# Three of four pairs of pool tiles with 84 products of 260 columns in place of 96, from sums of u kept in DRAM

## The chip, the cores and the metric

The kernel runs on one core of a Trainium2 chip. A core has five engines that run side by side, each with its own queue of instructions: PE (matrix products), DVE (vector work), ACT (scalar functions and casts), POOL and SP; the last two issue most of the DMA transfers. Weights and inputs lie in DRAM, tiles in the on-chip SBUF (128 partitions), products in PSUM. The metric is the device time of one execution in microseconds (us).

## The reference

One layer of a hybrid decoder trunk works on 528 positions (16 learned ones, then 512 tokens) of 1024 channels. The normalized input is u. Its product with w_in gives the pool branch (1024 channels), the inputs of a Mamba-2 scan, and the gates. What the change touches is the pool branch: four groups of 256 channels, each averaged over its own window of past positions, minus the channel itself, then mixed by a 256 x 256 matrix:

```python
POOL_WINDOWS = (2, 4, 8, 16)
...
ug = u.reshape(bsz, seqlen, POOL_GROUPS, POOL_GROUP_DIM)
for g, win in enumerate(POOL_WINDOWS):
    xg = ug[:, :, g, :]
    cs = jnp.cumsum(xg.astype(jnp.float32), axis=1)
    ...
    mean = (cs - shifted) / count
    outs.append(mean.astype(u.dtype) - xg)
pooled = jnp.stack(outs, axis=2)
y = jnp.einsum("blgc,gcd->blgd", pooled, w_group)
```

In this text "u" inside pool_mixer is the product of the normalized input with the first 1024 columns of w_in; outside of it u is the normalized input itself. The scan's output and the pool's are each projected to 1024 channels, gated, added, multiplied by w_o, and followed by a squared-ReLU MLP and a last normalization.

## The kernel before

**Arithmetic.** All products are of fp32 accuracy: each operand is split into a high part (a cast to fp32r) and a low part (the rest), and each product is three matmuls, high by high, high by low, low by high. The weights come as blocks of 128 x 1024 (512 KB): `block` (L82) loads one on SP's queue into `raw` (three buffers), ACT casts it to `whi` (L79), DVE subtracts to get `wlo` (L80). `whi` and `wlo` have four buffers each, shared by all blocks in turn. u lies in SBUF as `uh` and `ul`, eight tiles of 128 channels each (k = 0 to 7). `proj` (L155) makes one output tile of 128 channels from one block: for each k the high weights by uh and ul, in two halves of the positions, then the low weights by uh: 8 x 2 x 3 = 48 matmuls.

**Order of the work.** The engines' order is set by the code's order as a scheduler has arranged it with its own costs; the order that results was read from the instruction list. The stages: projections of the first scan group; eight groups of the scan (`ssd`, L423), each woven step by step (`weave`, L553) with the projections of the next; the pool stage; the merge of the two branches (L775 on); w_o; MLP. Each scan group loads `abc`, 1 MB, on POOL's queue (L431).

**The pool stage (L628 to L695).** `pool_tile` (L628) makes one tile: the 48 matmuls into `pp` (PSUM, 258 to 264 columns a half, since a window of w needs w - 1 positions before the first token), a copy to SBUF by ACT (`pu`), additions of the tile to itself shifted by 1, 2, 4, ... (L641, DVE), the scaling and subtraction (L643), and the split of the result into `ph` (ACT, L647) and `pl` (DVE, L648). A group has two tiles, a pair. `pool_mix` (L651) multiplies a pair by the group's 256 x 256 weights (12 matmuls of 512 columns into `pg`), and splits the outcome into `yph` (ACT, L661) and `ypl` (DVE, L662). The groups go in the order 3, 2, 1, 0 (windows 16, 8, 4, 2). Between the tiles stand what fills PE: the last part of the scan's projection (`psl`, L676 to L679, whose sums DVE adds to `acc`), `gate_pool(7)` (L562) and the first `gate_ssd` (L666). Two groups share one block of mixing weights (`wgb`), which stays in its whi and wlo buffers while they last.

**The merge** (L775 on) loads, in each of its first six rounds, one block of w_o into SBUF (`wo_load`, L752) ahead of its other blocks, makes the next gate and the pool's up-projection `pup`, and forms gated sums on DVE.

PSUM: two buffers of two banks for the wide products (`psum2`), four of one bank for the narrow ones (`psum1`).

Of the kernel before, what the change touches and what calls it, by code (L numbers as in the profile page):

```python
# [9 lines left out]
F32 = mybir.dt.float32  # L10
# [4 lines left out]
P = 128  # L15
# [30 lines left out]
WARM = 9  # L46


@with_exitstack
def kernel(ctx: ExitStack, tc, xT, x, w, vec, fnw, out):  # L50
# [31 lines left out]
    def block():  # L82
        t = block_tiles()
        block_part(t, slice(0, 1024))
        return t[2:]

    def units():
# [335 lines left out]
    def ssd(g, cur):  # L423
# [6 lines left out]
        abc = gs.tile([P, R, SEQ], F32, tag="abc", name=f"abc{g}")  # L430
        nc.gpsimd.dma_start(abc, acs_d[hs, :].partition_broadcast(P))  # L431

# [69 lines left out]
        for c in range(3):  # L502
            dve.tensor_tensor(st[c + 1], st[c], bc(cdec[:, c, hs], 64), op=ALU.mult)
            dve.tensor_tensor(flat(st[c + 1]), flat(st[c + 1]), pv[c + 1], op=ALU.add)
        dve.tensor_tensor(dm, dm, cbm.unsqueeze(1).to_broadcast([P, R, 4, P]), op=ALU.mult)
        yield
# [43 lines left out]

    done = {}

# [48 lines left out]
    def out_part():  # L601

        un = units()
        for d in range(NK):
# [3 lines left out]
            yield  # L608

    for g in range(G):  # L610
        nxt = group_tiles(g + 1) if g + 1 < G else None
        fill = [group_proj(g + 1, nxt, GATE_AT.get(g))] if nxt else [out_part()]
        if g == 4:
            fill = [out_half()] + fill
        weave(ssd(g, cur), fill, 2 if g == 4 else 1)
        cur = nxt
    gc_stack.close()


# [3 lines left out]
    gp = pool_stack.enter_context(tc.tile_pool(name="gp", bufs=2, side="left", reuse_waits="tile"))  # L623
    wo_stack = ExitStack()
    wop = wo_stack.enter_context(tc.tile_pool(name="wop", bufs=1, side="right", reuse_waits="tile"))
    yps = {}

    def pool_tile(t):  # L628
        win = WIN[t // 2]
        ps = psum2(f"pp{t}")  # L630

        skip = min(NM - win, NM - 4)
        runs, view = wide(ps, skip)
        proj(runs, block(), U)
        u = gp.tile([P, L], F32, tag="pu", name=f"pu{t}")
        act.copy(u[:, skip:], view)
        s, wdt, lo_ = u, 1, skip
        while wdt < win:
            o = gp.tile([P, L], F32, tag="pw", name=f"pw{t}_{wdt}")
            lo2 = lo_ + wdt  # L640
            dve.tensor_tensor(o[:, lo2:], s[:, lo2:], s[:, lo_ : L - wdt], op=ALU.add)  # L641
            s, lo_, wdt = o, lo2, 2 * wdt
        dve.scalar_tensor_tensor(s[:, NM:], s[:, NM:], 1.0 / win, u[:, NM:],  # L643
                                 op0=ALU.mult, op1=ALU.subtract)
        ph = gp.tile([P, SEQ], F32R, tag="ph", name=f"ph{t}", bufs=3)
        pl_ = gp.tile([P, SEQ], F32R, tag="pl", name=f"pl{t}", bufs=3)
        act.copy(ph, s[:, NM:])  # L647
        dve.tensor_tensor(pl_, s[:, NM:], ph.bitcast(F32), op=ALU.subtract)  # L648
        return ph, pl_

    def pool_mix(gi, pooled, wgb):  # L651
# [14 lines left out]
    def gate_ssd(d):  # L666
# [4 lines left out]
        return gt  # L671

    pend = [pool_tile(2 * POOL_ORDER[0] + i) for i in range(2)]

    un = units()
    for d in range(NK):  # L676
        ps = psum2(f"psl{d}")[:, :SEQ]
        mm3s(ps, [(next(un), ys[k]) for k in (14, 15)])
        dve.tensor_tensor(acc[d], acc[d], ps, op=ALU.add)  # L679
    wgb = block()  # L680
    for n, gi in enumerate(POOL_ORDER):
        nxt = []
        if n < 3:
            nxt.append(pool_tile(2 * POOL_ORDER[n + 1]))
        if n == 0:
            gate_pool(NK - 1)
        if n == 3:
            gts = [gate_ssd(MERGE[0])]
        if n == 2:
            wgb = block()  # L690
        pool_mix(gi, pend, wgb)
        if n < 3:
            nxt.append(pool_tile(2 * POOL_ORDER[n + 1] + 1))
        pend = nxt
    pool_stack.close()  # L695


# [417 lines left out]
def _weight_blocks(i):  # L1115
# [9 lines left out]
    def put(b):  # L1125
        blocks.append(b)
# [34 lines left out]
    blocks += pieces((14, 15))  # L1161
    wg(POOL_ORDER[0] // 2)
    for n in range(4):
        if n < 3:
            put(cols(w_in, 2 * POOL_ORDER[n + 1] * P))
        if n == 0:
            gate(NK - 1)
        if n == 3:
            gate(NK + MERGE[0])
        if n == 2:  # L1170
            wg(POOL_ORDER[n] // 2)
        if n < 3:
            put(cols(w_in, (2 * POOL_ORDER[n + 1] + 1) * P))

# [7 lines left out]
    for n, d in enumerate(MERGE):  # L1182
        if n < len(WO_ORDER):
            wo(*WO_ORDER[n])
        if n + 1 < NK:
            gate(NK + MERGE[n + 1])
        put(cols(w_up, d * P))
    for i in range(2):
        wo("b21", i)
# [62 lines left out]
```

## Time and profile before

| what | us |
|---|---|
| median of 3 runs | 1017.89 (1017.77 to 1018.33) |
| the profiled execution | 1017.65 |
| its span | 1015.9 |
| PE busy | 1007.5 |
| DVE busy | 740.5 |
| ACT busy | 549.1 |
| POOL busy | 10.0 |

The span is the time between the profile's first and last instruction; 1.75 us of the profiled execution lie outside. Engines work at the same time, so busy times don't add up to the span. In lines of groups the columns are: line, engine, operation, output<-input with shapes, xcount | total busy us, mean ns of one | idle us ahead of them and what ended it. In lines of the timeline: start, duration, engine, line, operation, and in brackets the idle time just before and what ended it. Matmuls overlap, so what one costs is read from the distance of starts, not from its duration.

### The profile page before, as it was taken

Reading aid. Unit: us, or ns where it says so; the run is one execution under the profiler, and the core shown is the slowest. Engines: PE = TensorE matmul, PEld = TensorE weight load, DVE = VectorE, ACT = ScalarE, POOL = GpSimd, SP = SyncE. Lnnn points to the kernel's source line nnn. Section 1 sums busy time; section 2 is a strip of 40 time slices with the busy share of each in tenths; the row PEclk is TensorE's granted clock in tenths of the full one; section 3 lists DMA queues with packets and bytes.
Section 4 is the critical chain, followed back from the end, with each engine's and each line's share of the span. In section 5 each row is a group of like instructions: output and inputs, shape, how many; then the busy total and the mean of one; then the engine's idle time right before and its main releaser. Section 6 shows DMA issues by size and latency. Waiting matters only on the chain.

```text
span 1015.9 us, 14095 instructions
## 1 busy us (share of the span) xinstructions
PE 1007.5 (99%) x5697; PEld 869.4 (86%) x5697; DVE 740.5 (73%) x988; ACT 549.1 (54%) x725; POOL 10.0 (1%) x24
## 2 busy tenths in 40 slices
PE   9999999999999999999999999999999999999997
PEld 8889899999889999978999888888888888888886
DVE  7988787777746587887766457887676686676866
ACT  8675958585727339553244333465545455354444
POOL 0100000000000000000000001000000000000000
PEclk9999999999999999999999999999999999999999
DMA  7242242414233231414432334133333323324112
GB/s 249 80 164 84 63 145 63 145 35 154 79 100 113 83 105 42 158 52 138 172 96 91 105 97 151 42 117 133 104 100 108 104 83 125 103 84 125 42 42 84
DMA packets 29715, 105.64 MB, mean 104 GB/s; under 512 B 3345, under 2 KB 4689, under 8 KB 28625
## 3 DMA queue, kind: packets, MB, share of 16 engines
q1 hardware_dynamic: 26928, 92.75, 28.7%
q0 software_dynamic: 2000, 11.08, 2.9%
q8 instruction: 45, 0.74, 0.3%
q10 hardware_dynamic: 720, 0.91, 0.3%
q14 instruction: 22, 0.17, 0.1%
HBM read 102.55 MB, written 2.16 MB: 103 GB/s over the span
## 4 chain that ended last, share of the span: by engine, by line
PE 96%; DVE 2%; ACT 1%; DMA 0%; issue 0%; SPq 0%; ACTq 0%
PE px L161 11%; PE alpha L1000 6%; PE pf L98 6%; PE pf L97 6%; PE pf L100 6%; PE px L163 6%; PE pz L161 5%; PE alpha L1003 3%; PE pp L161 3%; PE pgp L161 3%; PE pgs L161 3%; PE pz L163 3%; PE py L518 2%; PE pso L97 2%; PE pp L163 1%; PE pgp L163 1%
## 5 line engine op out<-in xcount | busy, mean ns | idle before, releaser
L80 DVE TENSOR_TENSOR wlo<-raw,whi 128x1024 fp32r<-128x1024 f32 (+1 forms) x134 | 158.8, 1188 | 123.8 <-ACT whi L79 80.9
L79 ACT CAST whi<-raw 128x1024 fp32r<-128x1024 f32 (+1 forms) x134 | 136.6, 1025 | 202.6 <-PE pf L98 47.0
L161 PE MATMUL px<-uh,whi 128*128 128x264 f32 (+1 forms) x448 | 113.2, 291 | 0.0
L163 PE MATMUL px<-ul,whi 128*128 128x264 f32 (+1 forms) x448 | 110.4, 285 | 0.0
L97 PE MATMUL pf<-vh,whi 128*128 128x512 f32 x256 | 99.8, 390 | 0.0
L98 PE MATMUL pf<-vl,whi 128*128 128x512 f32 x256 | 99.6, 389 | 0.0
L161 PEld LDWEIGHTS px<-uh,whi 128*128 128x128 f32 x448 | 84.6, 189 | 2.2 <-issue 1.5
L163 PEld LDWEIGHTS px<-ul,whi 128*128 128x128 f32 x448 | 84.3, 188 | 0.3
L764 DVE TENSOR_TENSOR slo<-b,shi 128x1024 fp32r<-128x1024 f32 x35 | 42.6, 1218 | 28.8 <-ACT shi L763 15.2
L100 PE MATMUL pf<-vh,wlo 128*128 128x512 f32 x256 | 63.6, 389 | 0.0
L763 ACT CAST shi<-b 128x1024 fp32r<-128x1024 f32 x35 | 36.7, 1050 | 44.9 <-PE pf L98 30.2
L161 PE MATMUL px<-uh,wlo 128*128 128x264 f32 (+1 forms) x448 | 58.5, 283 | 0.0
L100 PEld LDWEIGHTS pf<-vh,wlo 128*128 128x128 f32 x256 | 48.0, 188 | 10.0
L97 PEld LDWEIGHTS pf<-vh,whi 128*128 128x128 f32 x256 | 48.1, 188 | 9.9
L98 PEld LDWEIGHTS pf<-vl,whi 128*128 128x128 f32 x256 | 48.0, 188 | 9.9
L161 PEld LDWEIGHTS px<-uh,wlo 128*128 128x128 f32 x448 | 55.9, 188 | 0.0
L1000 PE MATMUL alpha<-shi,hh 128*128 128x512 f32 x140 | 54.6, 390 | 0.0
L1003 PE MATMUL alpha<-shi,hl 128*128 128x512 f32 x140 | 54.5, 389 | 0.0
L830 DVE TENSOR_TENSOR ht<-ht,alpha 128x1024 f32<-128x1024 f32 x35 | 42.5, 1215 | 15.7 <-PE alpha L1000 15.7
L163 PE MATMUL pz<-ul,whi 128*128 128x512 f32 x112 | 43.6, 389 | 0.0
L161 PE MATMUL pz<-uh,whi 128*128 128x512 f32 x112 | 43.6, 389 | 0.0
L539 DVE RECIPROCAL rs<-rs 128x128 f32<-128x128 f32 x32 | 27.2, 911 | 15.1 <-ACT rs L537 15.1
(415 smaller groups left out, 2330.7 us busy)
## 6 DMA issues: line engine op xcount, KB each, us to landing
raw<-in_w SPq DMA_DIRECT2D x128, 512.0 KB, 3.6
b<-in_w SPq DMA_DIRECT2D x28, 512.0 KB, 3.6
abc<-acs_d POOLq DMA_DIRECT2D x8, 1024.0 KB, 6.2
wob<-in_w SPq DMA_DIRECT2D x8, 512.0 KB, 4.6
xt<-in_xT SPq DMA_DIRECT2D x8, 264.0 KB, 4.7
ht<-in_x POOLq DMA_DIRECT2D x4, 512.0 KB, 5.5
w<-in_w SPq DMA_DIRECT2D x4, 512.0 KB, 3.4
out_dram<-out SPq DMA_DIRECT2D x4, 320.0 KB, 2.5
```

The lines of the kernel that those rows point to most:

```text
L79: act.copy(hi[:, c], raw[:, c])
L80: dve.tensor_tensor(lo[:, c], raw[:, c], hi[:, c].bitcast(F32), op=ALU.subtract)
L97: pe.matmul(ps, ah, bh, start=first and n == 0, stop=False)
L98: pe.matmul(ps, ah, bl, start=False, stop=False)
L100: pe.matmul(ps, al, bh, start=False, stop=last and n == len(pairs) - 1)
L161: pe.matmul(o, wt, rhs[0][k][:, c], start=part == 0 and k == 0, stop=part == 1 and k == NK - 1)
L163: pe.matmul(o, wt, rhs[1][k][:, c], start=False, stop=False)
L763: act.copy(hi, src)
L764: dve.tensor_tensor(lo, src, hi.bitcast(F32), op=ALU.subtract)
L830: dve.tensor_tensor(o, o, src, op=op)
L1000: pe.matmul(ps[t], hh[:, p, seg, st], m, start=bool(first and not low and p == 0), stop=bool(last and low and p == 1), skip_group_check=True)
L1003: pe.matmul(ps[t], hl[:, p, seg, st], m, start=False, stop=False, skip_group_check=True)
```

## The change

Strassen's method (in Winograd's form) makes the product of two matrices, each cut into 2 x 2 blocks, with seven block products in place of eight. Here the left matrix is the weights of a pair (two tiles of 128 channels, the 1024 input channels cut into two halves), and the right one is u (two halves of the input channels, two halves of the positions). The pair of group 3 stays as it was; those of groups 2, 1 and 0 become `pool_pair`: seven products of 4 x 3 = 12 matmuls with 260 columns, 84 for 96. The tokens are cut at 8: positions 8 to 267 and 268 to 527.

The parts:

1. **Weights.** A pair's two blocks are loaded raw. DVE forms four sums of 512 columns, and four forms A, S, D (1024 columns) and B (512) are split into high and low as blocks are, through the same four whi and wlo buffers.
2. **Sums of u.** For each k of 0 to 3, four sums of quarters of u are needed, the same for all pairs. They are formed along the scan, one k in each of the groups 1 to 4: POOL adds high and low parts (two of 128 x 520, behind the group's abc load), DVE does four subtractions of 260 columns, ACT casts twice, DVE makes two lows, and four tiles of 266 KB are written to DRAM on POOL's queue. `ua`, `ub`, `th` and `tl` have one buffer each. After the scan, 16 loads on POOL's queue bring them back into a pool of their own, `tf`.
3. **Combining.** Partial products that several outputs share stay in PSUM (`pxx`, `pyz`) and are copied on the way: ACT does four copies of 260 columns, DVE three additions of 260 columns per pair. `averaged` is the window part of the old pool_tile.
4. **Order.** gate_pool(7) goes ahead of the pairs; the loads of w_o stand behind the gate's and the up-projection's blocks of a round, and their buffers open after the pool stage. The order of the weight blocks in DRAM follows.

By the instruction list PE has 36 matmuls fewer. In the pool stage PE's order after psl is: gate_pool(7), x·A of pair 2, the rest of pool_mix(3), y·A, x·S, z·S, x·D, z·D and x·B of pair 2, y·A and x·A of pair 1, the first two matmuls of pool_mix(2), x·S of pair 1, and so on. A name like x·S2 in the text below is the product into x with form S of pair 2.

```diff
+
+    def raw_block():
+        b = nblk[0]
+        nblk[0] += 1
+        t = wp.tile([P, 1024], F32, tag="raw", name=f"raw{b}", bufs=3)
+        nc.sync.dma_start(t, w[b])
+        return t
+    def split_form(src, c, name):
+        hi = wp.tile([P, 1024], F32R, tag="whi", name=f"whi{name}")
+        lo = wp.tile([P, 1024], F32R, tag="wlo", name=f"wlo{name}")
+        act.copy(hi[:, c], src[:, c])
+        dve.tensor_tensor(lo[:, c], src[:, c], hi[:, c].bitcast(F32), op=ALU.subtract)
+        return hi, lo
...
+    ts_stack = ExitStack()
+    tsp = ts_stack.enter_context(tc.tile_pool(name="tsp", bufs=1, side="right", reuse_waits="tile"))
+    t_d = {(n, p, k): dram.tile([P, 2 * TN], F32R, name=f"t_d{n}{p}{k}")
+           for n in ("13", "42") for p in "hl" for k in range(4)}
+    one, two = slice(0, TN), slice(TN, 2 * TN)
+    def sums_of_u(k, g):
+        a, b = (tsp.tile([P, 2 * TN], F32, tag=t, name=f"{t}{k}") for t in ("ua", "ub"))
+        with tc.issue_after(abc_load[g].ins):
+            for t, kk in ((a, k), (b, k + 4)):
+                pool.tensor_tensor(t, uh[kk][:, SKIP:L].bitcast(F32), ul[kk][:, SKIP:L].bitcast(F32), op=ALU.add)
+        yield
+        with tc.issue_after(masked[g].ins):
+            dve.tensor_tensor(a[:, one], a[:, two], a[:, one], op=ALU.subtract)
+            dve.tensor_tensor(a[:, two], b[:, two], a[:, two], op=ALU.subtract)
+            dve.tensor_tensor(b[:, two], b[:, two], a[:, one], op=ALU.subtract)
+            dve.tensor_tensor(b[:, one], b[:, one], b[:, two], op=ALU.subtract)
+        yield
+        for src, n in ((a, "13"), (b, "42")):
+            hi, lo = (tsp.tile([P, 2 * TN], F32R, tag=f"t{p}", name=f"t{p}{n}{k}") for p in "hl")
+            act.copy(hi, src)
+            dve.tensor_tensor(lo, src, hi.bitcast(F32), op=ALU.subtract)
+            nc.gpsimd.dma_start(t_d[n, "h", k], hi)
+            nc.gpsimd.dma_start(t_d[n, "l", k], lo)
+            yield
...
+        if 0 < g < 5:
+            fill.append(sums_of_u(g - 1, g))
...
-    wo_stack = ExitStack()
-    wop = wo_stack.enter_context(tc.tile_pool(name="wop", bufs=1, side="right", reuse_waits="tile"))
+    tf = pool_stack.enter_context(tc.tile_pool(name="tf", bufs=1, side="left", reuse_waits="tile"))
...
-        s, wdt, lo_ = u, 1, skip
+        return averaged(t, u)
+    def averaged(t, u):
+        win = WIN[t // 2]
+        s, wdt, lo_ = u, 1, min(NM - win, NM - 4)
...
+    def pool_pair(p):
+        a1, a2 = raw_block(), raw_block()
+        sm = tf.tile([P, 1024], F32, tag="sm", name=f"sm{p}")
+        h1, h2, both = slice(0, 512), slice(512, 1024), slice(0, 1024)
+        fa = split_form(a1, both, f"A{p}")
+        dve.tensor_tensor(sm[:, h1], a2[:, h1], a2[:, h2], op=ALU.add)
+        dve.tensor_tensor(sm[:, h2], sm[:, h1], a1[:, h1], op=ALU.subtract)
+        fs = split_form(sm, both, f"S{p}")
+        dve.tensor_tensor(a1[:, h1], a1[:, h1], a2[:, h1], op=ALU.subtract)
+        dve.tensor_tensor(a1[:, h2], a1[:, h2], sm[:, h2], op=ALU.subtract)
+        fd = split_form(a1, both, f"D{p}")
+        fb = split_form(a2, h2, f"B{p}")
+        r1, r2 = (gp.tile([P, L], F32, tag="pu", name=f"pu{2 * p + i}") for i in range(2))
+        n = POOL_ORDER.index(p) % 2
+        x, y, z = pxx[:, 512 * n : 512 * n + TN], pyz[:, :TN], pyz[:, 512 : 512 + TN]
+        c1, c2 = slice(SKIP, SKIP + TN), slice(SKIP + TN, L)
+        u1, u2 = (lambda k: (uh[k][:, c1], ul[k][:, c1])), (lambda k: (uh[k][:, c2], ul[k][:, c2]))
+        form = lambda n, c: lambda k: (T[n, "h", k][:, c], T[n, "l", k][:, c])
+        def product(ps, wf, c, f, start, stop, k0=0):
+            for low in range(2):
+                for k in range(4):
+                    wt = wf[low][:, 512 * c + k * P : 512 * c + (k + 1) * P]
+                    bh, bl = f(k0 + k)
+                    pe.matmul(ps, wt, bh, start=start and not low and k == 0, stop=stop and low == 1 and k == 3,
+                              skip_group_check=True)
+                    if not low:
+                        pe.matmul(ps, wt, bl, start=False, stop=False, skip_group_check=True)
+        product(x, fa, 0, u1, True, False)
+        act.copy(r1[:, c1], x)
+        product(y, fa, 1, u1, True, True, 4)
+        dve.tensor_tensor(r1[:, c1], r1[:, c1], y, op=ALU.add)
+        product(x, fs, 1, form("42", two), False, False)
+        act.copy(r1[:, c2], x)
+        product(z, fs, 0, form("13", one), True, False)
+        act.copy(r2[:, c2], z)
+        yield
+        product(x, fd, 0, form("13", two), False, False)
+        dve.tensor_tensor(r2[:, c2], r2[:, c2], x, op=ALU.add)
+        product(z, fd, 1, u2, False, True, 4)
+        dve.tensor_tensor(r1[:, c2], r1[:, c2], z, op=ALU.add)
+        first = averaged(2 * p, r1)
+        product(x, fb, 1, form("42", one), False, True)
+        act.copy(r2[:, c1], x)
+        yield [first, averaged(2 * p + 1, r2)]
 
...
+    T = {i: tf.tile([P, 2 * TN], F32R, name="t{}{}{}".format(*i)) for i in t_d}
+    for i, t in T.items():
+        nc.gpsimd.dma_start(t, t_d[i])
...
     wgb = block()
+    gate_pool(NK - 1)
+    pxx, pyz = psum2("pxx"), psum2("pyz")
     for n, gi in enumerate(POOL_ORDER):
-        nxt = []
         if n < 3:
-            nxt.append(pool_tile(2 * POOL_ORDER[n + 1]))
-        if n == 0:
-            gate_pool(NK - 1)
+            pair = pool_pair(POOL_ORDER[n + 1])
+            next(pair)
         if n == 3:
             gts = [gate_ssd(MERGE[0])]
         if n == 2:
             wgb = block()
         pool_mix(gi, pend, wgb)
         if n < 3:
-            nxt.append(pool_tile(2 * POOL_ORDER[n + 1] + 1))
-        pend = nxt
+            pend = next(pair)
...
+    wo_stack = ExitStack()
+    wop = wo_stack.enter_context(tc.tile_pool(name="wop", bufs=1, side="right", reuse_waits="tile"))
...
     for n, d in enumerate(MERGE):
-        if n < len(WO_ORDER):
-            wo_load(*WO_ORDER[n])
         if n + 1 < NK:
             gts.append(gate_ssd(MERGE[n + 1]))
         if n >= NK - 2:
             first.append(split(woq["b11", n - NK + 2]))
         ps = psum2(f"pup{d}")[:, :SEQ]
         wh, wl = block()
+        if n < len(WO_ORDER):
+            wo_load(*WO_ORDER[n])
         cs = [slice(k * P, (k + 1) * P) for k in ks]
         mm3s(ps, [((wh[:, c], wl[:, c]), yps[k]) for c, k in zip(cs, ks)])
```

More of the change, by code (lines that the diff above doesn't have):

```diff
@@ L46 @@
 WARM = 9
+SKIP = 8
+TN = (L - SKIP) // 2
 @with_exitstack
@@ L430, in ssd @@
         abc = gs.tile([P, R, SEQ], F32, tag="abc", name=f"abc{g}")
-        nc.gpsimd.dma_start(abc, acs_d[hs, :].partition_broadcast(P))
+        abc_load[g] = nc.gpsimd.dma_start(abc, acs_d[hs, :].partition_broadcast(P))
         xdt = gs.tile([P, 4, R, 64], F32, tag="xdt", name=f"xdt{g}")
@@ L504, in ssd @@
             dve.tensor_tensor(flat(st[c + 1]), flat(st[c + 1]), pv[c + 1], op=ALU.add)
-        dve.tensor_tensor(dm, dm, cbm.unsqueeze(1).to_broadcast([P, R, 4, P]), op=ALU.mult)
+        masked[g] = dve.tensor_tensor(dm, dm, cbm.unsqueeze(1).to_broadcast([P, R, 4, P]), op=ALU.mult)
         yield
@@ L549, in ssd @@
         yield
-    done = {}
+    done, abc_load, masked = {}, {}, {}
     def weave(a, b, n):
@@ L617 @@
     gc_stack.close()
+    ts_stack.close()
     gp_stack = ExitStack()
@@ L1162, in _weight_blocks @@
     wg(POOL_ORDER[0] // 2)
+    gate(NK - 1)
     for n in range(4):
         if n < 3:
-            put(cols(w_in, 2 * POOL_ORDER[n + 1] * P))
-        if n == 0:
-            gate(NK - 1)
+            for i in range(2):
+                put(cols(w_in, (2 * POOL_ORDER[n + 1] + i) * P))
         if n == 3:
@@ L1171, in _weight_blocks @@
             wg(POOL_ORDER[n] // 2)
-        if n < 3:
-            put(cols(w_in, (2 * POOL_ORDER[n + 1] + 1) * P))
     def wo(name, i):
@@ L1182, in _weight_blocks @@
     for n, d in enumerate(MERGE):
-        if n < len(WO_ORDER):
-            wo(*WO_ORDER[n])
         if n + 1 < NK:
@@ L1187, in _weight_blocks @@
         put(cols(w_up, d * P))
+        if n < len(WO_ORDER):
+            wo(*WO_ORDER[n])
     for i in range(2):
```

## Prediction

> **What bounds the kernel now.** I read the page's busy times and chain of waits first, then the list of PE's waits, then the windows of the two stages that the edit touches.
>
> ```profile
> span 1015.9 us, 14095 instructions
> PE 1007.5 (99%) x5697; PEld 869.4 (86%) x5697; DVE 740.5 (73%) x988; ACT 549.1 (54%) x725; POOL 10.0 (1%) x24
> PEclk9999999999999999999999999999999999999999
> PE 96%; DVE 2%; ACT 1%; DMA 0%; issue 0%; SPq 0%; ACTq 0%
> ```
>
> PE is busy for 99% of the span, at full clock in all forty slices, and the chain that ended last is 96% PE. The waits of PE agree, and the two windows show the stages:
>
> ```profile
> PE pdt L203 <- DVE ones_r L108: 1.5, 1, 1.5
> PE psp L97 <- ACT yh L546: 0.9, 1, 0.9
> PE pt_dt L342 <- DVE ddt L331: 0.2, 1, 0.2
> ```
> ```profile
> core 0: us, PE busy (x) PEld busy (x) DVE busy (x) ACT busy (x) POOL busy (x), PEclk, DMA share, GB/s
> 95.00:340.00 245.00, 244.98 (x1618) 219.21 (x1615) 179.67 (x270) 161.45 (x213) 2.65 (x5) 1.00 0.32 103
> 477.00:562.00 85.00, 85.00 (x556) 77.73 (x555) 53.45 (x69) 33.54 (x43) 0.00 (x0) 1.00 0.42 132
> ```
>
> In the whole run PE waits 2.6 us for other engines. In the pool stage (477 to 562 us) it never stops, DVE is busy 53 us of 85, ACT 34. So a matmul removed there is worth its pitch, as long as nothing PE needs comes later. DVE has the second most to do, and the edit gives it work in both stages.
>
> **What is removed.** The pitch of a pool matmul is read from starts: the first of a tile, its last group, and the first of the next work.
>
> ```profile
> 501.52 0.29 PE L161 MATMUL pp<-uh,whi 128*128 128x260 f32 x1
> ...
> 505.36 2.06 PE L161 MATMUL pp<-uh,wlo 128*128 128x260 f32 x16
> 507.26 0.40 PE L161 MATMUL pgp<-uh,whi 128*128 128x512 f32 x1
> ...
> 541.52 0.39 PE L97 MATMUL pg<-ph,whi 128*128 128x512 f32 x1
> 542.89 0.28 PE L161 MATMUL pp<-uh,whi 128*128 128x258 f32 x1
> ...
> 546.68 2.08 PE L161 MATMUL pp<-uh,wlo 128*128 128x258 f32 x16
> 548.60 0.39 PE L161 MATMUL pgs<-uh,whi 128*128 128x512 f32 x1
> ```
>
> A tile of 48 matmuls of 260 columns takes 507.26 - 501.52 = 5.74 us, 0.1196 each; of 258 columns 548.60 - 542.89 = 5.71, 0.119 each; the six 512-column ones from 541.52 to 542.89 take 0.228 each. Pair 2: 96 x 0.1196 - 84 x 0.1196 = 1.44 us saved. Pairs 1 and 0: 96 x 0.119 - 84 x 0.1196 = 1.38 each. **Removed: 4.2 us.** The count of twelve per pair and the pitch are both plain, so 3.9 to 4.2 bounds it. The 12 matmuls of each pool_mix, the gate and the out-part stay; gate_pool(7) only changes place.
>
> **What is added to DVE and ACT in the pool stage.** Here are prices from the stage's own groups (count, then busy total and mean in ns) and, for pitch, from starts that follow each other.
>
> ```profile
> 483.97 1.23 DVE L80 TENSOR_TENSOR wlo<-raw,whi 128x1024 fp32r<-128x1024 f32 x1 [4.07 <-ACT whi L79]
> 485.11 0.70 DVE L641 TENSOR_TENSOR pw<-pu 128x527 f32<-128x527 f32 x1
> 485.84 2.17 DVE L641 TENSOR_TENSOR pw<-pw 128x525 f32<-128x525 f32 x3
> 488.05 0.69 DVE L643 SCALAR_TENSOR_TENSOR pw<-pw,pu 128x512 f32<-128x512 f32 x1
> ...
> 499.28 1.28 DVE L679 TENSOR_TENSOR acc<-acc,psl 128x512 f32<-128x512 f32 x2
> ```
> ```profile
> L662 DVE SCALAR_TENSOR_TENSOR ypl<-pg,vs,yph 128x512 fp32r<-128x512 f32 x8 | 5.9, 747 | 1.0 <-ACT yph L661 1.0
> L504 DVE TENSOR_TENSOR st<-st,pst 128x256 f32<-128x256 f32 x24 | 9.9, 412 | 0.2
> L79 ACT CAST whi<-raw 128x1024 fp32r<-128x1024 f32 x16 | 16.8, 1052 | 38.0 <-PE pp L163 14.6 <-PE psl L98 8.6 <-issue 8.0
> L647 ACT CAST ph<-pw 128x512 fp32r<-128x512 f32 x8 | 5.0, 619 | 7.3 <-DVE pw L643 7.3
> L498 ACT COPY st<-pst 128x256 f32<-128x256 f32 x8 | 2.9, 366 | 1.4 <-PE pst L496 1.4
> ```
>
> A 1024-column low costs DVE 485.11 - 483.97 = 1.14; a 512-column add 0.72 when it follows its own input (2.17 / 3) and about 0.61 when not (1.28 - 0.69 = 0.59 is the second of two adds); a 260-column add from PSUM has no row of its own: the 256-column one lasts 0.41 with its tail, of which about 0.07 overlaps the next, as it does with the two adds; I take 0.34 (0.30 to 0.41). ACT: 1.05, 0.62 and 0.37.
>
> For a pair the old code asked of DVE two 1024 lows, the window sums and the lows of ph and yph. The new one asks: three 1024 lows and a 512 low, 3 x 1.14 + 0.61 = 4.0; four 512 sums of weights, 2.4; three adds of 260, 1.0; window sums, some 3.9 for pair 1; two lows of ph 1.2; two ypl 1.4; one low of the pool weights 1.14 for every second pair. That is 14 to 15 us a pair. PE's share of a pair is now 84 x 0.1196 + 12 x 0.228 = 12.8 us. **So DVE, not PE, is the slower engine over pairs 2 and 1**, and it cannot work ahead freely: whi and wlo have four buffers, and one holds the pool weights of groups 3 and 2 until pool_mix(2), so three rotate. S1's forms (S of pair 1) go where D2's were, D1's where B2's were, B1's where A1's were.
>
> **The largest wait.** I count from the start of y·A2 (t = 0); a product is 12 x 0.1196 = 1.435 us. PE's order, as the instruction list has it: y·A2, x·S2, z·S2 (ends 4.3), x·D2, z·D2, x·B2 (8.6), y·A1 and x·A1 (11.5, with a copy before the second 11.65), then pg2 from ph4, the first averaged tile of pair 2, queued ahead of x·S1. On DVE: the buffer of S2 is free at 4.0, ACT casts A1 (1.05), so A1's low starts at 5.1. From there to ph4's input, in DVE's order: low of A1 1.14, add of x 0.34, two sums for D1 1.21, add of z 0.34, low of S1 1.14, first window sum 0.61: 9.9. Low of D1 1.14 (its cast is done 1.05 after x·B2's last use, 9.65), second window sum 0.61: 11.65. The low of B1 waits for x·A1 to leave its buffer, 11.8, and takes 0.61; third window sum 0.61, the scaling of L643 0.69 and its tail: 13.9. The cast of ph4 on ACT is 0.62: 14.6. **PE waits 14.6 - 11.65 = 2.95 us.** Behind this matmul stand x·S1 and all of pair 1, though they need nothing of ph4; no earlier work is left.
>
> The same list for the next pair: pair 1's window sums are one addition shorter, but its two ypl, delayed by the first stall, stand in front. Resuming at 14.6, PE reaches pg1 from ph2 at 28.6 (six products, two times 0.46 and 2.8 of pg2, then x·A0 and y·A0); DVE's list to ph2 ends between 30.0 and 30.7: a wait of 1.4 to 2.1, I take 1.6. Pair 0's mix has the first gate_ssd in front (24 x 0.228 = 5.5 us): none.
>
> **Smaller new waits.** x of pair 0 is written where pair 1's x·B1 is still being copied, or to the other half of the same tile: a copy of 0.37 and the hand-overs, 0.6 to 0.9, taken 0.75. x·A1 behind a copy 0.15. psl, where adds now stand behind two sums of weights of 0.61 and 0.72, has a wait of 0.29 already on the loading side:
>
> ```profile
> 492.52 0.19 PEld L97 LDWEIGHTS psl<-yh,whi 128*128 128x128 f32 x1 [0.29 <-DVE acc L679]
> ```
>
> I add 0.3. Pool stage: -4.2 + 2.95 + 1.6 + 0.75 + 0.15 + 0.3 = **+1.55**.
>
> **The scan.** In each of groups 1 to 4 DVE gets four subtractions of 260 columns and two lows of 520 (4 x 0.34 + 2 x 0.63 = 2.6 us) and ACT two casts (1.2). Over 245 us that is 10.5 and 5 us on engines with 65 and 83 us free (the first window), so nearly all hides. It isn't free where PE's queue waits on DVE with no slack:
>
> ```profile
> 112.63 0.88 DVE L474 TENSOR_SCALAR abc<-abc,dtok 128x128 f32<-128x128 f32 x4 [3.45 <-ACT eb L466]
> 113.42 0.40 DVE L446 TENSOR_TENSOR xdtm<-ptm,dtm 16x256 f32<-16x256 f32 x1
> ```
>
> DVE runs such stretches back to back. Eight additions of 128x520 go to POOL, whose row nearest to it and that of DVE are
>
> ```profile
> L641 DVE TENSOR_TENSOR pw<-pw 128x517 f32<-128x517 f32 x2 | 1.4, 697 | 0.1
> L110 POOL TENSOR_SCALAR_AFFINE_SELECT tri<-ones_f 128x128 f32<-128x128 f32 x1 | 0.3, 283 | 0.0
> ```
>
> so 0.70 to 0.283 x 520 / 128 = 1.15 each; POOL has nothing else to do, so the adds themselves are hidden. On POOL's queue, though, stand the abc loads too, and now 16 writes of 266 KB:
>
> ```profile
> 236.71 0.53 POOL L431 DMA_DIRECT2D abc<-acs_d  x1 [48.03 <-DVE xc L371]
> 241.49 1.06 ACT L529 ACTIVATE sqg<-yt 128x1024 f32<-128x1024 f32 x1
> ...
> 245.11 0.62 ACT L273 CAST qhg<-sqg 128x512 fp32r<-128x512 f32 x1 [1.85 <-DVE sqg L530]
> ```
> ```profile
> abc<-acs_d POOLq DMA_DIRECT2D x8, 1024.0 KB, 6.2
> out_dram<-out SPq DMA_DIRECT2D x4, 320.0 KB, 2.5
> ```
>
> th and tl have one buffer each, so the cast of t42 waits in ACT's queue until the write of t13 has landed. Nearest prices: 2.5 us (320 KB) and 6.2 (1 MB). In group 3 the cast of t13 stands ahead of sqg, so it ends at about 241.49 + 0.62 = 242.1, and its write goes out behind an abc load: landed at 242.1 + 2.5 = 244.6 or + 6.2 = 248.3, while ACT's next work that PE needs is at 245.11. Late by 0 to 3.2 us; the same again in group 4 at worst. I take the price of the transfer of its size, so 0, and 0.9 for DVE's dense stretches (0 to 1.5: a third of the 2.6 us in one group, or nothing).
>
> The T loads (16 x 266 KB at the page's rates, some 2.5 us each and overlapping) end around 486 us, 25 us before x·S2; the wo loads behind the pool stage still come three or more blocks ahead of their sums. Cost 0; if a T load were late PE would wait for it once, in x·S2.
>
> **Sum.** The profiled execution took 1017.65 us, 1.75 outside its span. -4.2 + 5.75 + 0.9 = +2.45: 1020.1. The median of the runs, 1017.89, lies 0.24 above the profiled one, so 1020.34, **forecast 1020.3 us**.
>
> **Rivals.**
> 1. Faster: DVE keeps up. If the scheduler's order costs less than I count (a low at 1.0 instead of 1.14, or a window sum run before the lows) ph4 and ph2 come in time and the matmuls count in full: 1017.9 - 4.2 + 0.2 of small waits = 1013.9. It decides for faster when all new waits are under 2.1 us. For it: DVE was idle for 31 of 85 us. Against: the idle time lay in waits for buffers, and those are now more.
> 2. The writes land late: 3.2 us at group 3 and up to as much at group 4: 1020.3 + 3 to 6.4, 1023 to 1027. For it: abc's 6.2 us in front on the same queue. Against: the out writes' 2.5.
> 3. POOL's additions hold DVE up. The Trainium skill, "SBUF — State Buffer", section "SBUF: two separate sides", says that DVE with two SBUF inputs and a GpSimd instruction that reads SBUF exclude each other for a whole instruction. As a mechanism here: eight additions of 1.15 us or more would stop DVE for their length in dense stretches; 8 x 1.15 = 9 us, of which perhaps a quarter reaches PE: 1020.3 + 2.3 = 1022.6. The trace has no POOL addition to judge it by. By the cost table of "GPSIMD Engine Reference", section 3.1, one would be an estimated 1.2 us. No run here shows that either.
> 4. The clock drops after the wait of 2.95 us. At the start nine 512-column matmuls run slowly:
>
> ```profile
> 1.51 4.21 PE L203 MATMUL pdt<-ones_r 128*128 128x512 f32 x9 [1.51 <-DVE ones_r L108]
> 5.67 0.89 PE L150 MATMUL px<-xh,whi 128*128 128x264 f32 x2
> ```
>
> They take (5.67 - 1.51) / 9 = 0.46 us each, twice 0.228. Such a stretch of 4.2 us costs 2.1: 1022.4. The Trainium skill, "TensorE: Matmul & The Clock Gate", Part 1, puts the drop behind an idle window of about 3.4 us; by it a wait of 2.95 would not suffice.
>
> **Chances.** Forecast 0.64 (its own range 1018.7 to 1021.7, from the 1.4 to 2.1, the 0 to 1.5 and the small waits); rival 1 0.09; rival 2 0.12; rival 3 0.10; rival 4 0.05. A measurement tells about 0.2% from no change, 2.04 us: faster is below 1015.85, slower above 1019.93. Rival 1 alone is faster: 0.09. Of the forecast's 0.64 some 0.27 lies below 1019.93, so same 0.27, slower 0.64. The range, 1017.8 to 1024.5, leaves out rival 1 and the upper half of rival 2: 0.15 to 0.2.
>
> **What would show it.** In the profile of the changed kernel PE's list of waits should name pg from ph (the cast), 2 to 3 us once and 1 to 2 once, with DVE busy without a gap before it; the 260-column matmuls should keep the pitch of 0.12, with 36 fewer matmuls. A wait on t42's cast or on qhg in groups 3 and 4 would speak for rival 2; DVE additions much over 0.7 us beside POOL's for rival 3; a PEclk digit below 9 near 525 us for rival 4. No wait of PE at pg, and the forecast is wrong in its main term.

## The result and the profile after

The changed kernel takes 1028.01 us (median of 6 runs, 1024.12 to 1030.26) against 1018.0 (6 runs, 1017.58 to 1018.55): ratio 1.0095, 95% interval 1.0075 to 1.0116. It is slower, as forecast, but by 10.0 us and not by 2.4, above the end of the range (1024.5). It also scatters over 6.1 us where the kernel before scatters over 1.0. The profiled execution, 1030.26 us, is the slowest of the six.

The same lines of the page, after:

```profile
span 1028.5 us, 14191 instructions
PE 1010.4 (98%) x5661; PEld 869.4 (85%) x5661; DVE 773.1 (75%) x1039; ACT 559.0 (54%) x746; POOL 38.7 (4%) x64
PEclk9999999999989999999999999999999999999999
PE 46%; ACT 0%; issue 0%; DVE 0%; ACTq 0%
```

There are 36 matmuls fewer (5661 for 5697), yet PE is busy for longer (1010.4 us for 1007.5), and the clock row has an 8 in its twelfth slice. Fewer matmuls and more busy time go together only if some of them ran slower. Six lines of PE's list of waits are new; these are the longest of all, with the four longest new ones among them:

```profile
PE pg L114 <- ACT ph L700: 4.1, 2, 2.8
PE pso L114 <- ACT acc L615: 2.8, 1, 2.8
PE pdt L220 <- DVE ones_r L125: 1.5, 1, 1.5
PE ptx L470 <- DVE xdtm L463: 1.3, 1, 1.3
PE psp L114 <- ACT yh L563: 0.9, 1, 0.9
PE pxx L729 <- ACT pu L749: 0.7, 1, 0.7
```

The first and the last are in the pool stage, and they are the forecast's: 2.8 and 1.3 for ph4 and ph2 (it had 2.95 and 1.6), 0.7 behind the copy (0.75). The second and the fourth are in the scan. The two stages in windows, moved by what lies in front of them:

```profile
95.00:349.00 254.00, 249.50 (x1620) 221.51 (x1617) 197.35 (x294) 166.59 (x222) 22.90 (x29) 0.99 0.36 116
486.00:575.00 89.00, 84.15 (x522) 75.88 (x521) 68.31 (x96) 38.44 (x56) 0.00 (x0) 0.98 0.41 135
```

DVE is now busy for 68 us of 89 in the pool stage. The scan's product py, after the second wait, starts at 286.60 us before and 295.43 after; the first gate behind the pairs at 548.60 and 561.14. So 8.8 us are lost by 295 us, nearly all in the scan (0.4 is a wait at 8 us, in the first projections), and 12.5 - 8.8 = 3.7 behind it, in the pool stage. Before, then after:

```profile
286.60 1.09 PE L518 MATMUL py<-abc,xdt 128*64 128x128 f32 x16
```
```profile
295.43 0.99 PE L535 MATMUL py<-abc,xdt 128*64 128x128 f32 x14
561.14 0.40 PE L178 MATMUL pgs<-uh,whi 128*128 128x512 f32 x1
```

(The line of the gate before, 548.60, stands in the prediction.) Of the 8.8, 3.0 are there ahead of the wait in group 4 (po starts at 283.09 for 280.08), 2.8 are that wait, and 3.0 come behind it.

**The wait in group 4.** The timeline of ACT, then PE, around 280 us:

```profile
278.32 0.63 ACT L651 CAST th<-ua 128x520 fp32r<-128x520 f32 x1
281.51 1.05 ACT L82 CAST whi<-raw 128x1024 fp32r<-128x1024 f32 x1 [2.56 <-PE pso L115]
285.80 0.62 ACT L651 CAST th<-ub 128x520 fp32r<-128x520 f32 x1 [3.23 <-DMA t_d13h<-th]
286.32 0.58 ACT L615 COPY acc<-pso 128x512 f32<-128x512 f32 x1
```
```profile
283.09 1.06 PE L529 MATMUL po<-ct,st 128*128 128x128 f32 x8
286.96 0.80 PE L114 MATMUL pso<-yh,whi 128*128 128x512 f32 x1 [2.81 <-ACT acc L615]
287.55 0.63 PE L115 MATMUL pso<-yl,whi 128*128 128x512 f32 x1
287.98 0.63 PE L114 MATMUL pso<-yh,whi 128*128 128x512 f32 x1
...
293.04 0.39 PE L114 MATMUL pso<-yh,whi 128*128 128x512 f32 x1
```

ACT's second cast of the group waits for the DRAM write of the first, because th has one buffer; behind it in ACT's queue stands the copy that empties pso's PSUM tile, and PE waits for that. The write was issued at 279.25 us and had not landed before 285.7, 6.4 us in all. The forecast took the price of the 320 KB writes, 2.5, and kept 6.2 for a rival, which had the write behind an abc load. Here the last abc load was issued at 239.09, 40 us earlier, so that is not the reason. After the wait the matmuls of 512 columns start 0.43 us apart (287.55, 287.98), not 0.23, until 293.0.

**The clock.** The windows view around the two longest waits; the column behind POOL's is the granted clock:

```profile
280.00:284.00 4.00, 4.00 (x23) 3.40 (x21) 1.88 (x4) 1.05 (x1) 0.53 (x1) 1.00 0.95 259
284.00:287.00 3.00, 0.19 (x3) 0.04 (x1) 1.62 (x3) 1.11 (x2) 0.29 (x1) 0.85 0.61 188
287.00:293.00 6.00, 6.00 (x14) 4.74 (x15) 0.25 (x1) 0.00 (x0) 0.78 (x2) 0.50 0.35 114
531.00:534.00 3.00, 0.17 (x3) 0.00 (x1) 2.62 (x5) 0.67 (x2) 0.00 (x0) 1.00 0.64 176
534.00:537.00 3.00, 3.00 (x17) 2.91 (x18) 3.00 (x6) 0.44 (x2) 0.00 (x0) 0.72 0.51 173
537.00:545.00 8.00, 8.00 (x52) 7.57 (x52) 5.96 (x9) 4.48 (x8) 0.00 (x0) 0.89 0.00 0
```

From 287 to 293 us PE runs at half clock; behind the wait for ph4 part of 534 to 537 and of 537 to 545 does (3 x 0.28 + 8 x 0.11 = 1.7 us lost). In the first stretch it is 3 x 0.15 + 6 x 0.50 = 3.4 us, of which 0.4 falls into the wait itself and 3.0 on matmuls. The page's clock row keeps its 9 at the second stretch: there 1.7 us are lost in a slice of 26, so the digit that the prediction named as a sign is too coarse to show it.

**POOL's additions.** DVE's instruction that runs beside the first two of them, against the same one of the kernel before:

```profile
96.12 1.31 POOL L641 TENSOR_TENSOR ua<-uh,ul 128x520 f32<-128x520 f32 x1
97.39 1.32 POOL L641 TENSOR_TENSOR ub<-uh,ul 128x520 f32<-128x520 f32 x1
...
96.21 3.05 DVE L542 TENSOR_TENSOR yt<-yt,zt 128x512 f32<-128x512 f32 x1
```
```profile
96.10 0.68 DVE L525 TENSOR_TENSOR yt<-yt,zt 128x512 f32<-128x512 f32 x1
```

3.05 us in place of 0.68: the addition ends at 99.26, 0.55 us after POOL's second one (98.71), so it got nearly all of its work done only then, and DVE's whole queue is 2.4 us late. PE's wait of 1.3 us for xdtm comes 18 us later; that the two belong together is tested below (adds on DVE). The Trainium skill, "SBUF — State Buffer", section "SBUF: two separate sides", has the rule as the prediction's third rival told it, and the trace agrees: the two exclude each other for the whole instruction.

### The profile page after: what moved, and what is told of

It is laid out like the page before. It is cut to its first block, busy times and chain, and to the rows that moved or that the text cites. A ratio compares the mean times of both kernels' runs of the same rounds, so it can differ in the third digit from the quotient of the medians.

```text
span 1028.5 us, 14191 instructions
## 1 busy us (share of the span) xinstructions
PE 1010.4 (98%) x5661; PEld 869.4 (85%) x5661; DVE 773.1 (75%) x1039; ACT 559.0 (54%) x746; POOL 38.7 (4%) x64
## 5 line engine op out<-in xcount | busy, mean ns | idle before, releaser
L82 ACT CAST whi<-raw 128x1024 fp32r<-128x1024 f32 (+1 forms) x128 | 130.3, 1024 | 180.9 <-PE pf L115 47.0
L83 DVE TENSOR_TENSOR wlo<-raw,whi 128x1024 fp32r<-128x1024 f32 (+1 forms) x128 | 153.9, 1206 | 99.4 <-ACT whi L82 63.8
L1105 PE MATMUL alpha<-slo,hh 128*128 128x512 f32 x140 | 37.4, 389 | 0.0
```

What stands on the lines that cost most here:

```text
L82: act.copy(hi[:, c], raw[:, c])
L83: dve.tensor_tensor(lo[:, c], raw[:, c], hi[:, c].bitcast(F32), op=ALU.subtract)
L1105: pe.matmul(ps[t], hh[:, p, seg, st], m, start=bool(first and not low and p == 0), stop=bool(last and low and p == 1), skip_group_check=True)
```

## Experiments

Theory A, from the two traces: POOL's additions hold DVE up, the late landing of a write holds ACT up, PE at half clock follows long waits, and the pool stage's waits are the forecast's. Theory B: the additional work of DVE and ACT hides in the scan as forecast, and the pool stage holds the loss. All runs are against the kernel before on the same chip, and the differences below are those from it, since it varies by 0.4 us from chip to chip (the changed kernel: +10.0). The scan and the pool stage were first taken apart.

| kernel | us, median (lowest to highest) | before | ratio, 95% interval |
|---|---|---|---|
| sums alone | 1024.07 (1022.29 to 1024.63) | 1017.58 | 1.0059, 1.0046 to 1.0072 |
| pool alone | 1021.90 (1020.66 to 1022.84) | 1017.58 | 1.0041, 1.0029 to 1.0053 |
| own buffers | 1023.23 (1022.37 to 1023.67) | 1017.58 | 1.0054, 1.0042 to 1.0066 |
| adds on DVE | 1025.95 (1022.16 to 1027.19) | 1017.58 | 1.0076, 1.0063 to 1.0090 |
| scan mended | 1021.62 (1021.09 to 1023.38) | 1017.90 | 1.0040, 1.0027 to 1.0054 |
| mix after s | 1022.60 (1021.36 to 1023.41) | 1017.90 | 1.0047, 1.0034 to 1.0059 |
| filled wait | 1020.97 (1020.59 to 1021.60) | 1017.90 | 1.0031, 1.0020 to 1.0043 |
| mix last | 1022.29 (1022.13 to 1023.07) | 1017.90 | 1.0045, 1.0032 to 1.0058 |
| four pu | 1018.39 (1017.54 to 1018.54) | 1017.76 | 1.0005, 0.9996 to 1.0014 |
| two pairs | 1017.01 (1016.58 to 1017.49) | 1017.76 | 0.9993, 0.9984 to 1.0002 |
| two pairs, groups 1 3 4 5 | 1016.64 (1016.33 to 1017.32) | 1017.74 | 0.9990, 0.9981 to 0.9999 |
| four pu, groups 1 3 4 5 | 1018.38 (1017.87 to 1019.23) | 1017.74 | 1.0007, 0.9998 to 1.0016 |

### Sums alone

The kernel before, with `sums_of_u` along the scan; T isn't loaded and the pool stage is the old one.

> The kernel before with the sums of u formed along the scan and written to DRAM, and nothing that uses them (the loads after the scan are left out, the pool stage is the old one). Theory A: the scan's loss is made of three things that the profile of the changed kernel shows: POOL's eight additions stop DVE for 1.3 to 1.5 us each (some 3 us reach PE), the cast of t42 in group 4 waits for a landing (2.8 us of PE), and TensorE then runs at half rate for one or two windows of 3.4 us (1.7 or 3.4 us lost). So 1024 to 1027 us. Theory B (the forecast's): the extra DVE and ACT work hides but for 0.9 us, and the rest of the loss belongs to the pool stage: 1018.9 us.

1024.07, 6.5 us over before. Theory A's figures hold and B's (1018.9) doesn't: the greater part of the loss is in the scan. The waits of PE in it:

```profile
PE pso L100 <- ACT acc L601: 2.6, 1, 2.6
...
PE ptx L456 <- DVE xdtm L449: 1.3, 1, 1.3
```

Both are those of the changed kernel.

### Pool alone

No sums are formed: the parts of u themselves are written to DRAM in their place, so the products are of the right size and of other numbers.

```diff
     def sums_of_u(k, g):
...
+        for kk, n in ((k, "13"), (k + 4, "42")):
+            nc.gpsimd.dma_start(t_d[n, "h", k], uh[kk][:, SKIP:L])
+            nc.gpsimd.dma_start(t_d[n, "l", k], ul[kk][:, SKIP:L])
```

> The changed kernel without the sums: the parts of u themselves are written to DRAM in the place of the sums (so the products use other numbers), with no work of POOL, DVE or ACT for them. Theory A: the scan loses nothing, the pool stage has -4.2 of matmuls, 4.8 to 5.6 of waits and 1.7 of half rate when a window follows the 2.8 us wait: 1018.6 to 1021.5 us. Theory B: the pool stage holds most of the loss: over 1024 us.

1021.90, 4.3 us over before, 0.4 above A's end and below B's. With the 6.5 of the sums alone that makes 10.8, against 10.0 measured together: the two losses add up to within the scatter, and the pool stage's is the smaller. Its waits are those of the changed kernel, and the clock behind them too (0.97 over 60 us is 1.8 us of full speed):

```profile
PE pg L114 <- ACT ph L687: 4.1, 2, 2.8
...
PE pxx L716 <- ACT pu L736: 0.7, 1, 0.7
```
```profile
500.00:560.00 60.00, 55.20 (x350) 50.26 (x350) 48.10 (x70) 28.90 (x43) 0.00 (x0) 0.97 0.32 101
```

### Own buffers, and adds on DVE

Two edits to the scan, one at a time. Own buffers: th13 and th42 have a buffer each, the lows are formed in place.

```diff
-            hi, lo = (tsp.tile([P, 2 * TN], F32R, tag=f"t{p}", ...) for p in "hl")
+            hi, lo = tsp.tile([P, 2 * TN], F32R, tag=f"th{n}", ...), src.bitcast(F32R)
```

> The changed kernel with a buffer of its own for each of the four tiles that are written to DRAM in a group (the lows are formed in place in ua and ub), so that no cast waits for a landing within a group. Theory A: PE's wait of 2.8 us before pso goes, and with it the half rate behind it (3.4 us): 1020 to 1023.5 us, and the half-rate stretch in the scan is gone from the records. Theory B: the cast was late for other reasons and PE waits as long elsewhere: 1026 to 1029 us.

1023.23, within A's figures: +5.65 for +10.0. No line for pso is left in PE's waits, and the clock stays at 1.00 where the half-rate stretch stood:

```profile
260.00:300.00 40.00, 40.00 (x205) 32.93 (x204) 26.15 (x41) 20.77 (x32) 2.15 (x4) 1.00 0.39 119
```

Adds on DVE: `pool.tensor_tensor` becomes `dve.tensor_tensor` in the first loop of sums_of_u.

> The changed kernel with the eight additions of 128x520 on DVE in place of POOL. Theory A: they cost DVE 8 x 0.61 = 4.9 us in place of the 10 to 11 us for which POOL's stop it, DVE's instructions in the scan keep their usual length (no 3 us ones), and 1 to 2 of the 3 us of small waits go: 1024 to 1027.5 us with the wait in group 4 still there. Theory B: DVE's load is what delays PE, so more of it on DVE costs more: 1028.5 to 1032 us.

1025.95, within A's figures: +8.4 for +10.0, where B had it slower. With more work on DVE the kernel is no slower, and in the median faster, though it scatters by 5 us, so that the 1.6 us between the medians is a rough figure. The instruction beside which POOL worked has its old length, and the line for ptx is gone from PE's waits, while pso's stays:

```profile
96.00 0.68 DVE L542 TENSOR_TENSOR yt<-yt,zt 128x512 f32<-128x512 f32 x1
```
```profile
PE pso L114 <- ACT acc L615: 2.5, 1, 2.5
PE pdt L220 <- DVE ones_r L125: 1.5, 1, 1.5
PE psp L114 <- ACT yh L563: 0.9, 1, 0.9
```

### Scan mended

Both edits together.

> The changed kernel with both edits to the sums at once: the eight additions on DVE, and a buffer of its own for each tile that is written. Theory A: the scan then costs as good as nothing, and what is left is the pool stage as it was alone (+4.3 us): 1021.0 to 1022.5 us, one half-rate stretch of 3.4 us, behind the 2.8 us wait for ph4. Theory B: DVE's and ACT's extra work in the scan costs something by itself: over 1023 us.

1021.62: A's figure, +3.7 for +10.0. But its profile isn't as A had it, in two ways. The scan isn't free: group 4's py starts 1.3 us later than before (287.94 for 286.60; 0.4 of it is the wait at 8 us), and PE's list has a new wait of 1.1 us behind DVE's st (L521). Both edits together make one, for the lows now lie in ua and ub, and DVE's next addition into ua has to wait for the write of the last one to land:

```profile
158.06 0.70 DVE L641 TENSOR_TENSOR ua<-uh,ul 128x520 f32<-128x520 f32 x1 [3.96 <-DMA t_d13l<-ua]
```

In adds on DVE the same addition waits for nothing and there is no wait behind st, which fits; no run tests it. And the profile has the 2.8 us wait for ph4 and no half rate behind it:

```profile
500.00:560.00 60.00, 55.22 (x356) 49.88 (x356) 49.55 (x72) 29.38 (x44) 0.00 (x0) 1.00 0.32 105
```

So a wait of this length may or may not bring the half rate; the last section shows what decides.

### Mix after s, mix last, four pu

Three steps on what bounds the pool stage. The first two queue pool_mix of pairs 2 and 1 later on PE; `mark` is the last matmul of z·S of the next pair in the one, of x·B in the other (which also puts a pair's first window sums behind its last copy in the code):

```diff
+            with tc.issue_after(mark.ins):
                 pool_mix(gi, pend, wgb)
```

> The kernel of scan_mended with the mix of pair 2 (and of pair 1) queued on PE behind z.S of the next pair, 2.9 us later than before. If DVE is the slower engine over the pair, as the forecast says, the wait only moves to ph5, whose list on DVE ends some 3 us behind PE: 1020 to 1022 us, a wait of 2 to 3.5 us for ph5. If only the place of the first two matmuls of the mix was at fault, the waits for ph4 and ph2 go with nothing in their place: 1015.5 to 1017.5 us.

> The kernel of scan_mended with the mix of pair 2 (and of pair 1) queued on PE behind all seven products of the next pair, 7.2 us later than before. If DVE's lag behind PE over a pair is about 2 to 3 us and is made good by the gate's matmuls ahead of pair 0's mix, the waits for ph go: 1017.6 - 4.2 + 1 to 2 of small waits, 1014.4 to 1016.5 us, no half rate. If the forms of weights come late in place of ph (DVE is behind with everything), waits of over 2 us show at the products of pairs 1 and 0: 1018 to 1021 us.

1022.60 and 1022.29: no gain at all. In both the waits for ph are gone and waits of about the same sum stand elsewhere. Mix after s, then mix last:

```profile
PE pxx L729 <- ACT pu L736: 4.6, 2, 3.1
```
```profile
PE pxx L729 <- ACT pu L736: 3.1, 1, 3.1
...
PE pyz L729 <- ACT pu L742: 1.1, 1, 1.1
```

4.6 and 4.2 us in place of 4.1, now for copies of products into pu. The first of the two expectations had named ph5, and neither had named pu; that the wait moves and doesn't go was right. In mix last the copy has the cast of ph4 in front of it on ACT, and that waits for DVE's window sums:

```profile
525.35 0.62 ACT L700 CAST ph<-pw 128x512 fp32r<-128x512 f32 x1 [2.41 <-DVE pw L696]
525.87 0.37 ACT L736 COPY pu<-pxx 128x260 f32<-128x260 f32 x1
```

Four pu gives mix last two more buffers for pu (`bufs=4`).

> The kernel of mix_last with four buffers in place of two for pu, the tiles into which the products are copied. In mix_last PE waits 4.2 us for ACT's copies into pu, which wait until DVE's window sums have read the pair before. If that is only a matter of buffers, DVE's lag is now taken up by them and made good under the gate's matmuls: 1016.5 to 1018.3 us, no wait over 1 us in the pool stage. If DVE has more work than PE in these pairs, the wait moves on, to lows of weight forms or to ph: 1018.5 to 1021 us with waits of 2 us and more.

1018.39, between the two figures: +0.6 for mix last's +4.4. With the four buffers the first copies of the next pair no longer stand behind ph's cast (523.12, ahead of the cast at 525.84), and what remains are waits for DVE itself, none of them near the 2 us that the second figure asked for:

```profile
PE pyz L729 <- DVE pu L738: 0.8, 1, 0.8
PE pxx L729 <- DVE pu L745: 0.6, 1, 0.6
```

So DVE's lag can be taken up by buffers and made good later. The stage from its first psl to the first gate then takes 58.75 us (490.43 to 549.18), for 59.06 before (489.54 to 548.60): 0.3 less, of the 4.2 that were removed.

### Filled wait

Ten matmuls of 512 columns, used nowhere, ahead of pair 2's mix, in scan mended.

> The kernel of scan_mended with ten matmuls of 512 columns (2.3 us of PE, results used nowhere) queued ahead of the first two matmuls of pair 2's mix, where PE waits for 2.8 us. If the half rate follows from PE standing still, the stretch at half rate is gone and the kernel is 1.7 us faster than scan_mended though it does more: 1019.5 to 1020.8 us. If half rate and wait are unrelated, the time is that of scan_mended or up to 0.5 us longer.

1020.97, 0.65 us below scan mended though it does more, but not 1.7: no decision. The highest of the runs came down (1021.60 for 1023.38), which fits half-rate stretches that no longer occur; the lowest came down too (1020.59 for 1021.09), which they don't explain. Neither of the two profiled executions has such a stretch, so they can't be compared for it.

### Two pairs, and other groups for the sums

Two pairs is scan mended with pair 1 by the old pool_tile (and with PSUM tiles of its own for each new pair).

> The kernel of scan_mended with pair 1 made in the old way (96 matmuls, no forms), so that pairs 2 and 0 alone are made from seven products. The old pair asks some 10 us of DVE for 14 us of PE, so DVE makes up its lag of 2 to 3 us there. If the waits come from DVE's lag, the two of them for ph go, and the stage keeps -2.8 us of matmuls: 1016 to 1018 us. If they come from the order of PE's queue and not from DVE's load, one wait of 2 us or more stays at the first matmuls of a mix: 1018.5 to 1021 us.

1017.01, 0.75 us below before (the interval reaches 1.0002). None of the three waits of the pool stage is left, and over 60 us PE stands still for 0.05:

```profile
500.00:560.00 60.00, 59.95 (x387) 54.19 (x387) 46.35 (x65) 30.10 (x43) 0.00 (x0) 1.00 0.41 132
```

The last two kernels form the sums in groups 1, 3, 4 and 5 of the scan (`if g in (1, 3, 4, 5)`).

> The kernel of two_pairs with the sums of u formed along the scan groups 1, 3, 4 and 5 in place of 1, 2, 3 and 4. In two_pairs the scan's only new wait stands in group 2 (po behind DVE's st, 0.6 us, and the row before it). If DVE is without slack there alone, the wait goes: 1016.0 to 1016.8 us, faster than the kernel before. If group 5 is as tight, the wait only moves: 1016.8 to 1017.3 us.

> The kernel of four_pu (all three pairs) with the sums along groups 1, 3, 4 and 5. The same step: 0.6 to 0.9 us less than four_pu's 1018.4, so 1017.5 to 1017.8 us; and, if DVE's load in the pool stage is what eats the third pair's gain, it stays behind the kernel with two pairs by 1 us or more, though it has 12 matmuls fewer.

1016.64 with two pairs, the one kernel that is faster than before beyond its interval (0.9981 to 0.9999, 1.1 us); 1018.38 with three, no change. The reason given was not met: the wait of po is still there, 0.6 us in the first, and so is DVE's wait for a landing (3.5 us at 157), so the step from 1017.01 to 1016.64 isn't explained and is within what two measurements can differ by. With three pairs the kernel is 1.7 us slower though it has 12 matmuls fewer, as expected; but the two also differ in the place of the mix and in the buffers for pu, so that the 1.7 is not the price of the third pair alone.

## Why the prediction was too small

- **What is removed, 4.2 us: right.** The new products keep the pitch: in two pairs the 84 of pair 2 run from 509.17 to 519.90 us, with three matmuls of the mix (0.68) among them, so 10.05 us or 0.1196 each, as forecast. Not all of it arrives: two pairs are worth 2.8, and from the first psl to the first gate the stage takes 57.19 us (490.15 to 547.34) for 59.06, 1.9 less. A wait of 0.3 at psl is part of the difference; the rest is spread over many hand-overs.
- **The pool stage's waits, 5.75 us: right in place and about in size.** 2.8, 1.3 and 0.7 for 2.95, 1.6 and 0.75. That DVE, not PE, is the slower engine over pairs 2 and 1 was argued from counts. Mix after s and mix last bear it out, since the wait moved with its size, and two pairs does the other way round, since with DVE's share lowered the waits are gone. But order and buffers count as well: four pu leaves DVE its work and has no wait over 0.8 us in the stage. Too small were the other small waits, 0.45 in the sum: scan mended's stage, without half rate, is 2.5 us longer than before (61.59 us from the first psl to the first gate), for 1.55 forecast, though its long waits were a little shorter than forecast.
- **The scan, 0.9 us: this step failed.** It measured 8.8 in the profiled execution (with the half rate, 3.0 of it), 6.5 in the median of the sums alone. Two of its statements were wrong. "The adds themselves are hidden" looked at POOL's time alone: DVE pays, 2.4 us for the first two, and some 2 us reach PE (adds on DVE: 1.6 in the median; in the profiled execution PE is 3.0 late ahead of the wait in group 4, from this and other causes). And for the landing, "I take the price of the transfer of its size, so 0": the write in group 4 took 6.4 us, in a stretch where the DMA engines were 95% busy (the window 280 to 284), and PE lost 2.8 us (own buffers). One median was the wrong price for 16 writes whose landings go from 2.3 to 6.4 us; the rival had the 6.2, with a chance of 0.12. Why this one was late isn't shown: the busy engines are an obvious candidate, but in group 3 writes of the same size landed in 3.1 and 3.2 us while the engines were as busy (a share of 0.95 and 0.82, for 0.78 here, each over the time of the write).
- **The clock after the waits: not in the sum, a chance of 0.05.** The changed kernel has 3.4 + 1.7 us of it in the profiled execution. I let the Trainium skill's 3.4 us of idleness talk down waits of 2.8; the runs say otherwise, see the last section. The size, 2.1 for one stretch, was not far off: one of 3.4 us costs up to 1.7, the double one cost 3.0 on matmuls.
- **The rivals were set up as alternatives.** Rivals 2, 3 and 4 came true together, and each had been priced on the forecast alone. (Rival 2 did in its effect, a late landing that holds up ACT, but in group 4 alone and not behind an abc load.) They are linked: the late write is the wait that brings the half rate. Added up at the forecast's own prices, 3.0 + 2.3 + 2 x 2.1 on 1020.3 would have been 1029.8.

What stays open: why the write in group 4 landed late, and the small new hand-overs of the pool stage (1 to 2 us).

## What to carry to other kernels

Moving work to an idle engine isn't free when its instructions keep another from its operands: compare the length of that engine's instructions beside the moved ones. A single buffer that is read by a DMA puts the landing time of the worst moment, not the usual one, into the queue of the engine that writes it next: ACT in the changed kernel, DVE when the lows moved into ua and ub. And when PE is bound, count the other engines per stage: of the kernels tried, the one that gained had two of three pairs made by Strassen's method and less work for DVE in the pool stage.

## What was not expected of the hardware

A wait of 2.5 to 3.1 us can be enough for a stretch at half rate: in the profiles it follows in 8 of 10 such waits, for 3.4 us each but once, when it was twice that (286.1 to 293.0 us). Between the first 8 us and PE's last matmul no profile has one without such a wait. The Trainium skill, "TensorE: Matmul & The Clock Gate", Part 1, names a window of about 3.4 us without work; the stretch has that length, the waits ahead of it were shorter. Such a wait can thus cost 1.4 to 3.0 us of matmul time on top of its length, and a kernel with several of them scatters: the mean granted clock of the changed kernel's runs goes from 0.998 in the fastest (1024.12 us) to 0.994 in the slowest (1030.26), which makes some 4 of the 6.1 us between them.

What decides can be read from the clock records of the traces. Within an execution every change of the clock falls on one grid of 3.413 us (in the changed kernel, 286.13 and 535.30 are 73 steps apart). What counted was how long PE stood still within one step of that grid, and the half rate began with the next step. Here are two steps of the changed kernel, then two of scan mended, around the same wait of 2.8 us:

```profile
531.89:535.30 3.41, 1.30 (x9) 1.22 (x10) 3.30 (x7) 0.89 (x2) 0.00 (x0) 1.00 0.70 249
535.30:538.71 3.41, 3.41 (x19) 3.41 (x17) 2.72 (x5) 0.53 (x2) 0.00 (x0) 0.50 0.10 38
```
```profile
525.01:528.42 3.41, 1.71 (x12) 1.62 (x13) 3.30 (x7) 0.89 (x2) 0.00 (x0) 1.00 0.73 253
528.42:531.83 3.41, 3.41 (x27) 3.30 (x27) 3.15 (x5) 2.22 (x4) 0.00 (x0) 1.00 0.00 0
```

PE stood still for 2.11 of 3.41 us in the first, and the clock halved; in the second the same wait lay across two steps, 1.70 us in the longer part, and it didn't. In the eight waits with half rate behind them the step had 1.98 to 2.69 us of standing still; in all other steps at full clock, in all 14 profiles, it was 1.70 or less. The double stretch fits: its wait reached 0.83 us into the first step at half rate, and another such step followed; the others reached 0.57 us or less into theirs. The grid lies differently in every execution, so the same wait brings the half rate in some and not in others. This is read from the traces; no run moved a wait along the grid.

The addition of 128x520 on POOL took 1.31 to 1.79 us (the forecast had 1.15 to 1.2), the one on DVE 0.70:

```profile
L641 POOL TENSOR_TENSOR ua<-uh,ul 128x520 f32<-128x520 f32 x4 | 5.9, 1474 | 0.1
```
```profile
L641 DVE TENSOR_TENSOR ua<-uh,ul 128x520 f32<-128x520 f32 x3 | 2.1, 698 | 4.1 <-DMA t_d13l<-ua 4.1
```
